# Low parts of 24 of layer 1's projection weights formed during layer 0 and kept in DRAM

## The chip, the cores and the metric

One core of a Trainium2 chip runs the whole kernel. The metric is device time in microseconds (us), less is better. The core has a matrix engine (PE), a vector engine (DVE), a scalar engine (ACT), GpSimd (POOL) and SyncE (SP), which here only issues transfers. Each engine works through its own queue in order, and they wait for one another by semaphores.

## The reference

A two-layer trunk over 256 latent and 256 context tokens of width 1024, in float32. Each layer, cut to what matters here:

```
mod  = silu(c) @ w_ada                  # modulation vectors (scale, shift, gate)
h    = rms_norm(x) * (1 + scale) + shift
p    = h @ w_in                         # q, k, v of three mixers, gates
y_a  = gated_delta_net(p)               # chunked: triangular inverse, then a scan over chunks
y_b  = B * dwconv3(C * h_)              # short gated convolution
y_c  = neighbourhood_attention(p)
x   += gate * ((sum_i sigmoid(g_i) * (y_i @ w_p[i])) @ w_o)      # "merge", then w_o
x   += gate * conv_ffn(rms_norm(x))                              # up projection, conv, down
```

The output is the latent stream after two layers and a last norm.

## The kernel before, in words

**Products in three passes.** Every float32 weight tile is split into a high part (`whi`, rounded to the matrix engine's fp32r type) and a low part (`wlo` = weight minus high part); the activations are split likewise (`hh`, `hl`). A product is three matrix passes: whi·hh, whi·hl, wlo·hh (`mm3`, L175 to L177; the same in `short_conv`, L759). `wsplit` does it for one tile of 128x1024 elements: SP loads it into a buffer `wr` (L135, three buffers), ACT casts it to `whi` (L162), and DVE or POOL subtracts (`wlo`, L165). Every `LOE`-th tile's subtraction goes to POOL: in layer 1's projections every fourth. Layer 0 has three `whi`/`wlo` pairs there and layer 1 four, so the split of a tile starts when PE is done with the tile four (three) before it.

**Stages of a layer.** Projections of the delta net (tiles of `w_in`: k GK 12 to 15, v GV 20 to 23, q GQ 16 to 19), the short convolution's (SCT 24 to 35), the triangular inverse, the scan over chunks, attention, merge, w_o, up projection, down projection. In the profile before, layer 0 has the 24 steps of its merge at 415 to 612 us, `w_o` to 657 us, its up projection to 899 us and its down projection (last tile `pcut`) to 1023 us; layer 1's projections, inverse and scan are at 1026 to 1225 us.

**The inverse.** `X` is formed from the Gram matrices of k (on PE), scaled, transposed into `Bk`; then 30 steps on DVE, each a product into `tm` (L687) and a sum into `Bk` (L688); then a transpose into `Tl` (L689), which the products `py` on PE (L739) read. The compiler weaves other DVE work between these steps: the convolutions of v and q (L350, L351), q's rotation (L522 to L525), the short convolution (`uu`, `cv`), and low parts `wlo`. Meanwhile PE works at the projections of v, q and the short convolution.

**Modulation.** `mod` is not a matrix product after the first part: `ada_all` loads tiles of 512 KB of `w_ada` into two buffers `araw` (L140), one tile ahead, and DVE multiplies and sums each (`aprod`, L241, two per tile). `ada_to` paces these: `ADT` = (0, 32, 16, 32) tiles in layer 0's merge (24 steps, one per block j and branch), up projection (22 steps) and down projection.

**Order.** A scheduler of the program decides the order on each engine from the program's order and the buffers; SP has one queue for nearly all loads. A load whose buffer is not free stands at the queue's head and holds what is behind it.

The step of the merge that paces the work is

```
ps = proj(GT + 3 * j + br, NA_)            # gate, 24 matmuls
w  = wsplit(w_p[l, j, br], 4)              # half a tile
mm3(py[:, OW], w, yhl[br][0], ...)         # pyp, 12 matmuls
ada_to(ADT[0] + (3 * j + bi + 1) * ADT[1] // 24)
```

Of the kernel before, what the change touches and what calls it, by code (L numbers as in the profile page):

```python
# [9 lines left out]
F32 = mybir.dt.float32  # L10
F32R = mybir.dt.float32r
AF = mybir.ActivationFunctionType
ALU = mybir.AluOpType
# [3 lines left out]
P = 128  # L17
# [43 lines left out]
PRE = (12, 13, 14, 15, 20, 21)  # L61

ADT = (0, 32, 16, 32)

CTO, CTD = (2, 0), 1
NC0, NUP, HLE = 4, 2, 0
# [15 lines left out]
def trunk(ctx, tc, xin, cin, cbin, con, par, w_ad0, w_ada, w_in, w_ab, bias, w_p, w_o, w_up, w_dn, out, dbg=None):  # L82
# [62 lines left out]

    cb, wsp = [], []

    def wsplit(src, k, m=128, pool=None, bufs=None, dst=None):
        raw = wraw(src.rearrange("p a b -> p (a b)"), k * m, "wr").rearrange("p (a b) -> p a b", b=m)
        if pool is None:  # L150
            pool, bufs = wsp[0]
        if dst is not None:
            hi, lo = dst
        else:
            hi = pool.tile([P, 8, 128], F32R, tag="whi", bufs=bufs, name="whi")[:, :k, :m]
            lo = pool.tile([P, 8, 128], F32R, tag="wlo", bufs=bufs, name="wlo")[:, :k, :m]
        lo_n[0] += 1
        E_ = G if lo_every[0] and lo_n[0] % lo_every[0] == 0 else V
        na, nb = cuts[0] if k == KD and m == P else (1, 1)
        for i in range(na):  # L160
            c = slice(i * k // na, (i + 1) * k // na)
            A.copy(hi[:, c], raw[:, c])  # L162
        for i in range(nb):
            c = slice(i * k // nb, (i + 1) * k // nb)
            E_.tensor_tensor(lo[:, c], raw[:, c], hi[:, c].bitcast(F32), ALU.subtract)  # L165
        return hi, lo

    def split(hi, lo, src):
        A.copy(hi, src)
        V.tensor_tensor(lo, src, hi.bitcast(F32), ALU.subtract)  # L170
# [84 lines left out]
    def ada_to(n):  # L255

        if not ada_on:
            ada_on.append(1)
            next(ada_gen)
        while ada_at[0] < n:  # L260
            next(ada_gen)
            ada_at[0] += 1
# [105 lines left out]
    for l in range(L):  # L368
# [15 lines left out]

        adf = {}

        def before(q):
            if l == 0:
                if q == 0:
                    adf[0] = ada_first(0, a0p)  # L390
                    next(adf[0])
                next(adf[q])
                if q == 3:
                    nc.sync.dma_start(cb[0], cbin)
                    A.activation(cb[0], cb[0], AF.Silu)
                if q < 3:
                    adf[q + 1] = ada_first(q + 1, a0p)
                    next(adf[q + 1])
            if q == QW[l]:
                raw = wraw(w_ab[l].rearrange("p a b -> p (a b)"), KD * 16, "wr").rearrange("p (a b) -> p a b", b=16)  # L400
                A.copy(wab[:, :, 0:16], raw)
                V.tensor_tensor(wab[:, :, 16:32], raw, wab[:, :, 0:16].bitcast(F32), ALU.subtract)
                for i in range(NT[l]):
                    pre[GK + i] = wsplit(w_in[l, GK + i], KD)
            if q == QX and l == 0:
                for i in range(NT[l], NT[l] + NPX):
                    pre[PRE[i]] = wsplit(w_in[l, PRE[i]], KD, pool=s0p, bufs=NPX)


        first = {}  # L410
# [55 lines left out]
        def proj(ti, n, name="prj", bank=pbank):  # L466
            if ti in first:
                return first.pop(ti)
            w = pre.pop(ti) if ti in pre else wsplit(w_in[l, ti], KD)
            ps = bank(name)  # L470
            mm3(ps[:, : n.stop - n.start], w, hh, hl, KD, n, True, True)
            return ps
# [279 lines left out]

        def short_conv():
            def fproj(ti):
                hi, lo = wsplit(w_in[l, ti], KD)
                ps = pbank("prj")
                for k in range(KD):
                    for i, (a, b) in enumerate(((hi, hh), (hi, hl), (lo, hh))):
                        mm = PE.matmul(ps[:, OW], a[:, k, :], b[:, k, NA_], start=k == 0 and i == 0, stop=k == KD - 1 and i == 2)  # L759
                        if in_scan[0]:  # L760
                            tc.keep_in_program_order(mm)
                        yield ps

            for i in range(4):
                cg = tmp("cg")
                for ps in fproj(SCT + 3 * i):
                    yield
                A.copy(cg[:, OW], ps[:, OW])
                for ps in fproj(SCT + 3 * i + 1):
                    yield  # L770
                uu = tmp("uu")
                V.tensor_tensor(uu[:, OW], ps[:, OW], cg[:, OW], ALU.mult)
                cv = tmp("cv")
                conv3(cv[:, OW].rearrange("p (s t) -> p s t", t=T), uu, lambda tap: pcol(l, "scc", tap * 4 + i), ns)
                for ps in fproj(SCT + 3 * i + 2):
                    yield
                V.tensor_tensor(y_b[:, i], ps[:, OW], cv[:, OW], ALU.mult)
# [199 lines left out]
        with left("at", l) as at:  # L977
            for i in range(4):
# [23 lines left out]
                if i % 2 == 0:  # L1002

                    vh = at.tile([P, 2, KD, P], F32R, tag="vh", bufs=1, name="vh")
                    vl = at.tile([P, 2, KD, P], F32R, tag="vl", bufs=1, name="vl")

                    vst = [wp.tile([P, 2, 4, P], F32R, tag="araw", bufs=2, name="vst") for _ in range(2)]
                    for a in range(2):
                        wsplit(w_in[l, NV + i + a], KD, dst=(vh[:, a], vl[:, a]))
                    for b in range(4):  # L1010
                        ps = pbank("pv")
                        n = slice(b * P, b * P + P)
                        for k in range(KD):
                            PE.matmul(ps[:, : 2 * P], hh[:, k, n], vh[:, :, k, :], start=k == 0, stop=False)
                            PE.matmul(ps[:, : 2 * P], hl[:, k, n], vh[:, :, k, :], start=False, stop=False)
                            PE.matmul(ps[:, : 2 * P], hh[:, k, n], vl[:, :, k, :], start=False, stop=k == KD - 1)
                        pv, vs = ps[:, : 2 * P].rearrange("p (h d) -> p h d", d=64), vst[b // 2][:, b % 2]
                        A.copy(vs[:, :, 0:64], pv)
                        V.tensor_tensor(vs[:, :, 64:P], pv, vs[:, :, 0:64].bitcast(F32), ALU.subtract)
# [57 lines left out]
        for j in range(KD):  # L1077
            acc = tmp("acc")
            for bi, br in enumerate(BRO):
                ps = proj(GT + 3 * j + br, NA_)  # L1080
                gt = tmp("gt", "tg")[:, OW]
                A.activation(gt, ps[:, OW], AF.Sigmoid)
                w = wsplit(w_p[l, j, br], 4)
                if j == 0 and (not last or br == 2 or YSP[br] > 3):
                    ysplit(br)
                py = gbank("pyp")
                mm3(py[:, OW], w, yhl[br][0], yhl[br][1], 4, OW, True, True)
                if bi == 0:
                    V.tensor_tensor(acc[:, OW], py[:, OW], gt, ALU.mult)
                else:  # L1090
                    V.tensor_tensor(gt, py[:, OW], gt, ALU.mult)
                    V.tensor_tensor(acc[:, OW], acc[:, OW], gt, ALU.add)
                if l == 0:
                    ada_to(ADT[0] + (3 * j + bi + 1) * ADT[1] // 24)
            split(mh[:, j], ml[:, j], acc[:, OW])
        RX.close()

# [50 lines left out]
        with right("f", l) as fp:  # L1148
# [22 lines left out]
            for i in range(FT):  # L1171
# [13 lines left out]
                split(fh[:, i], fl[:, i], uv[0])  # L1185
                if not last:
                    ada_to(sum(ADT[:2]) + (i + 1) * ADT[2] // FT)
            cut = 0 if last else CTD
            stat = Stat((fp.tile([P, NW], F32, tag="u", bufs=6, name="sa") if l == 1 else tmp("sa", "tg")), NA_, cut or None)
            norm = None if last else Norm(stat, x, l + 1, "n1g", 1, 0, hh, hl)  # L1190
# [9 lines left out]
            for j in range(KD):  # L1200
                if j == KD - 1 and cut:
                    ada_to(sum(ADT))
                    w = dsplit(j)
                    last_tiles([j], lambda ps, j, n: dmm(ps, j, n, w), 5, norm)
                    break
                ps = pbank("pdn")
                for (k0, kn) in dks:
                    w = wsplit(w_dn[l, j][:, k0 : k0 + kn], kn)
                    mm3(ps[:, OW], w, fh[:, k0 : k0 + kn], fl[:, k0 : k0 + kn], kn, OW, k0 == 0, k0 == 16)
                if not last:  # L1210
                    ada_to(sum(ADT[:3]) + (j + 1) * ADT[3] // KD)
                residual(ps, j, 5, NA_)
                stat.add(x, j)
                if last:
                    A.activation(x[:, j, LAT], x[:, j, LAT], AF.Copy, scale=pcol(0, "fng", j))
# [138 lines left out]
```

## Time and profile before

| | before |
|---|---|
| median of 3 runs | 1673.89 us (1673.30 to 1676.83) |
| profiled execution | 1671.71 us, span 1669.8 us |
| PE busy | 1593.0 us (95%) |
| DVE busy | 1173.2 us (70%) |
| ACT busy | 775.5 us (46%) |
| POOL busy | 232.4 us (14%) |
| mean granted PE clock | 0.977 of full speed |

The span runs from the first to the last instruction of the profiled execution; its time has 1.9 us more around it. The profiled execution lies 2.2 us below the median of the runs.

### The profile page before, as it was taken

What the parts mean: (1) busy time and instruction counts of PE and PEld (TensorE: products, weight loads), DVE (VectorE), ACT (ScalarE), POOL (GpSimd) and SP (SyncE); (2) the same over time, 40 slices, a digit from 0 to 9 for tenths busy, and PEclk for the clock granted to TensorE, in tenths of its full rate; (3) what the DMA queues carried; (4) which work ended last, traced back from release to release, by engine and by line L of the source; (5) the groups of instructions that cost most, each with busy time, mean ns of one, the idle gap of its engine ahead of it and who ended that gap; (6) DMA issues with size and microseconds to landing.
All of it is one profiled execution on the core that took longest, in us unless ns stands there. A gap on an engine that the chain in (4) does not pass through costs nothing.

```text
span 1669.8 us, 26300 instructions
## 1 busy us (share of the span) xinstructions
PE 1593.0 (95%) x10184; PEld 1365.1 (82%) x10184; DVE 1173.2 (70%) x2279; ACT 775.5 (46%) x1361; POOL 232.4 (14%) x181
## 2 busy tenths in 40 slices
PE   5999999999799999999999999979999999999997
PEld 4777788887588888888888888668798899989997
DVE  4697853777777766877778666796767765678753
ACT  3664533566322234544443224653356554466653
POOL 0100311000000000000000001212333033334442
PEclk9999999999899999999999999997999999999999
DMA  9221012312556552444445773122024156546653
GB/s 369 77 76 52 14 51 89 121 36 73 193 173 199 179 177 76 139 130 136 126 130 174 255 227 126 51 89 89 26 87 139 55 169 185 177 153 186 183 174 114
DMA packets 65452, 220.03 MB, mean 132 GB/s; under 512 B 7280, under 2 KB 8688, under 8 KB 65200
## 3 DMA queue, kind: packets, MB, share of 16 engines
q1 hardware_dynamic: 64448, 214.20, 40.2%
q0 software_dynamic: 880, 4.16, 0.8%
q8 instruction: 80, 1.31, 0.3%
q14 instruction: 44, 0.36, 0.1%
HBM read 217.28 MB, written 1.05 MB: 131 GB/s over the span
## 4 chain that ended last, share of the span: by engine, by line
PE 80%; DVE 12%; ACT 4%; issue 2%; DMA 2%; POOL 0%; SPq 0%; DVEq 0%; ACTq 0%; POOLq 0%
PE pup L175 7%; PE pup L176 7%; PE pup L177 7%; PE prj L175 6%; PE prj L176 6%; PE prj L177 6%; PE prj L759 5%; PE pdn L176 3%; PE pdn L177 3%; PE pdn L175 3%; PE pa L787 2%; PE pyp L176 2%; PE pyp L177 2%; PE pyp L175 2%; PE po L787 2%
## 5 line engine op out<-in xcount | busy, mean ns | idle before, releaser
L162 ACT CAST whi<-wr 128x1024 fp32r<-128x1024 f32 (+1 forms) x336 | 313.3, 935 | 505.2 <-PE prj L176 149.0
L165 DVE TENSOR_TENSOR wlo<-wr,whi 128x512 fp32r<-128x512 f32 (+2 forms) x340 | 292.2, 876 | 140.8 <-ACT whi L162 137.7
L175 PE MATMUL prj<-hh,whi 128*128 128x512 f32 (+1 forms) x736 | 261.0, 355 | 8.0 <-DVE v__8934 L351 2.5
L177 PE MATMUL prj<-hh,wlo 128*128 128x512 f32 (+1 forms) x736 | 260.8, 355 | 3.8 <-DVE wlo L165 3.8
L176 PE MATMUL prj<-hl,whi 128*128 128x512 f32 (+1 forms) x736 | 259.9, 353 | 0.0
L175 PE MATMUL pup<-hh,whi 128*128 128x256 f32 (+1 forms) x720 | 239.0, 334 | 1.4 <-ACT hh L340 1.4
L176 PE MATMUL pup<-hl,whi 128*128 128x256 f32 (+1 forms) x720 | 238.8, 333 | 0.0
L177 PE MATMUL pup<-hh,wlo 128*128 128x256 f32 (+1 forms) x720 | 238.7, 333 | 0.0
L165 POOL TENSOR_TENSOR wlo<-wr,whi 128x1024 fp32r<-128x1024 f32 (+2 forms) x80 | 163.7, 2046 | 371.2 <-ACT whi L162 345.9
L175 PEld LDWEIGHTS prj<-hh,whi 128*128 128x128 f32 x736 | 140.3, 191 | 28.1 <-ACT whi L162 3.5
L241 DVE SCALAR_TENSOR_TENSOR aprod<-araw,cb 128x1024 bf16<-128x1024 f32 x128 | 153.4, 1219 | 13.7 <-DMA araw<-w_ada 13.4
L177 PEld LDWEIGHTS prj<-hh,wlo 128*128 128x128 f32 x736 | 140.1, 190 | 23.6 <-DVE wlo L165 4.7
L176 PEld LDWEIGHTS prj<-hl,whi 128*128 128x128 f32 x736 | 140.1, 190 | 19.3 <-issue 3.0
L175 PEld LDWEIGHTS pup<-hh,whi 128*128 128x128 f32 x720 | 136.9, 191 | 14.9 <-ACT hh L340 1.8
L176 PEld LDWEIGHTS pup<-hl,whi 128*128 128x128 f32 x720 | 136.8, 191 | 13.2
L177 PEld LDWEIGHTS pup<-hh,wlo 128*128 128x128 f32 x720 | 136.9, 191 | 13.0
L176 PE MATMUL pdn<-fl,whi 128*128 128x256 f32 (+1 forms) x330 | 109.8, 333 | 0.0
L175 PE MATMUL pdn<-fh,whi 128*128 128x256 f32 (+1 forms) x330 | 109.7, 332 | 0.0
L177 PE MATMUL pdn<-fh,wlo 128*128 128x256 f32 (+1 forms) x330 | 109.7, 332 | 0.0
L497 POOL MEMSET wt<- 128x512 f32 x4 | 2.0, 526 | 697.9 <-PE pcut L176 645.5
L350 DVE SCALAR_TENSOR_TENSOR u<-pup,par,u 128x510 f32<-128x510 f32 (+1 forms) x88 | 53.6, 612 | 47.4 <-ACT u L349 47.4
L759 PE MATMUL prj<-hh,whi 128*128 128x512 f32 (+1 forms) x192 | 69.9, 364 | 0.3 <-DVE q__8924 L351 0.3
(344 smaller groups left out, 3193.3 us busy)
## 6 DMA issues: line engine op xcount, KB each, us to landing
wr<-w_in SPq DMA_DIRECT2D x128, 512.0 KB, 3.8
wr<-w_up SPq DMA_DIRECT2D x88, 512.0 KB, 3.6
araw<-w_ada SPq DMA_DIRECT2D x80, 512.0 KB, 4.0
wr<-w_dn SPq DMA_DIRECT2D x32, 512.0 KB, 4.4
wr<-w_p SPq DMA_DIRECT2D x48, 256.0 KB, 2.7
a<-w_ad SPq DMA_DIRECT2D x16, 512.0 KB, 10.6
wr<-w_o SPq DMA_DIRECT2D x16, 512.0 KB, 3.9
wr<-w_dn SPq DMA_DIRECT2D x16, 384.0 KB, 3.4
```

The source lines that it names most:

```text
L162: A.copy(hi[:, c], raw[:, c])
L165: E_.tensor_tensor(lo[:, c], raw[:, c], hi[:, c].bitcast(F32), ALU.subtract)
L175: PE.matmul(ps, hi[:, i, :], xh[:, i, n], start=first and i == 0, stop=False)
L176: PE.matmul(ps, hi[:, i, :], xl[:, i, n], start=False, stop=False)
L177: mm = PE.matmul(ps, lo[:, i, :], xh[:, i, n], start=False, stop=last and i == k - 1)
L241: V.scalar_tensor_tensor(prod, nxt, 1.0, cb[0][:, i], ALU.mult, ALU.mult, accum_out=macc[:, i, b : b + 1])
L350: V.scalar_tensor_tensor(dst[:, :, 1:T], pv[:, :, 0 : T - 1], wc(0), dst[:, :, 1:T], ALU.mult, ALU.add)
L497: G.memset(t, 0.0)
L759: mm = PE.matmul(ps[:, OW], a[:, k, :], b[:, k, NA_], start=k == 0 and i == 0, stop=k == KD - 1 and i == 2)
L787: i_ = PE.matmul(*a, **k)
```

## The change

For 24 tiles of layer 1's `w_in` (list `LOD`) the low part is formed in layer 0. A generator `lo_all` takes a tile at a time: SP loads it into an `araw` buffer, ACT casts each half into a buffer `lh`, DVE subtracts each half in place, and POOL's queue stores the 512 KB into a DRAM tile `lod`. `LDT` = (0, 10, 14, 0) paces it: 10 tiles over the merge's 24 steps and 14 over the up projection's 22, each call just behind `ada_to`. In layer 1 these tiles go through `win`: SP loads the tile as before, ACT casts it to `whi`, and SP loads `wlo` from `lod`; there is no subtraction. They no longer advance the counter that sends every fourth subtraction to POOL.

```
+LOD = (12, 13, 14, 15, 20, 21, 22, 23, 16, 17, 18, 19) + tuple(range(24, 36))
+LDT = (0, 10, 14, 0)
...
+    def lo_all():
+
+        for ti in LOD:
+            yield
+            raw = araw(w_in[L - 1, ti].rearrange("p a b -> p (a b)"))
+            for i in range(2):
+                c = slice(512 * i, 512 * i + 512)
+                t = tmp("lh").bitcast(F32R)
+                A.copy(t, raw[:, c])
+                V.tensor_tensor(raw[:, c].bitcast(F32R), raw[:, c], t.bitcast(F32), ALU.subtract)
+            lod[ti] = tc.dram_tile([P, KD * P], F32, name=f"lod{ti}")
+            G.dma_start(lod[ti], raw)
+        yield
...
-    def wsplit(src, k, m=128, pool=None, bufs=None, dst=None):
+    def wsplit(src, k, m=128, pool=None, bufs=None, dst=None, lod_=None):
...
+        if lod_ is not None:
+            A.copy(hi, raw)
+            nc.sync.dma_start(lo.bitcast(F32), lod_.rearrange("p (a b) -> p a b", b=m))
+            return hi, lo
         lo_n[0] += 1
         E_ = G if lo_every[0] and lo_n[0] % lo_every[0] == 0 else V
...
+        def win(ti, **a):
+            return wsplit(w_in[l, ti], KD, lod_=lod.get(ti) if last else None, **a)
...
-            w = pre.pop(ti) if ti in pre else wsplit(w_in[l, ti], KD)
+            w = pre.pop(ti) if ti in pre else win(ti)
...
                     ada_to(ADT[0] + (3 * j + bi + 1) * ADT[1] // 24)
+                    lo_to(LDT[0] + (3 * j + bi + 1) * LDT[1] // 24)
...
                     ada_to(sum(ADT[:2]) + (i + 1) * ADT[2] // FT)
+                    lo_to(sum(LDT[:2]) + (i + 1) * LDT[2] // FT)
```

Three places in the engines' orders follow; the changed program's line numbers are about 30 higher (L138 is L135 before, L143 is L140, L195 is L165, L720 is L687, L721 is L688, L722 is L689).

SP's queue in layer 0's merge, before: loads of half tiles `w_p` and tiles `w_in` for the merge, and of `w_ada`.

```order
L140 DMA araw<-w_ada 128x1024 x2
L135 DMA wr<-w_p 128x512
L135 DMA wr<-w_in 128x1024
L140 DMA araw<-w_ada 128x1024 x2
L135 DMA wr<-w_p 128x512
L135 DMA wr<-w_in 128x1024
L135 DMA wr<-w_p 128x512
L135 DMA wr<-w_in 128x1024
```

The same place of the change.

```order
L143 DMA araw<-w_ada 128x1024 x2
L138 DMA wr<-w_p 128x512
L143 DMA araw<-w_in 128x1024
L138 DMA wr<-w_in 128x1024
L138 DMA wr<-w_p 128x512
L143 DMA araw<-w_ada 128x1024 x2
L138 DMA wr<-w_in 128x1024
L143 DMA araw<-w_ada 128x1024
```

The load `araw<-w_in` of a tile to be stored stands in the queue among the merge's own loads; the next loads of `w_ada` take the buffers in turn, and one of them waits for the store from that tile's buffer.

DVE in layer 1, at the end of the 30 steps of the inverse, before.

```order
L687 TENSOR_TENSOR tm<-Bk 128x210
L772 TENSOR_TENSOR uu<-prj,cg 128x256
L688 TENSOR_TENSOR Bk<-Bk,tm 128x10x21
L165 TENSOR_TENSOR wlo<-wr,whi 128x1024
L687 TENSOR_TENSOR tm<-Bk 128x198
L350 SCALAR_TENSOR_TENSOR cv<-uu,par_74,cv 128x255
L688 TENSOR_TENSOR Bk<-Bk,tm 128x9x22
L351 SCALAR_TENSOR_TENSOR cv<-uu,par_74,cv 128x255
L687 TENSOR_TENSOR tm<-Bk 128x184
L165 TENSOR_TENSOR wlo<-wr,whi 128x1024
L688 TENSOR_TENSOR Bk<-Bk,tm 128x8x23
```

The end of the same steps in the change, up to the transpose into `Tl`.

```order
L666 TENSOR_TENSOR attn<-gram,E 128x256
L721 TENSOR_TENSOR Bk<-Bk,tm 128x2x29
L666 TENSOR_TENSOR attn<-gram,E 128x256
L720 TENSOR_TENSOR tm<-Bk 128x30
L666 TENSOR_TENSOR attn<-gram,E 128x256
L721 TENSOR_TENSOR Bk<-Bk,tm 128x30
L805 TENSOR_TENSOR uu<-prj,cg 128x256
L722 STREAM_TRANSPOSE Tl<-Bk 128x32x32
```

All eight subtractions `wlo` between the 30 steps are gone; the Gram products' scaling (`attn`) and the second `uu`, which waits for a matmul of tile 28, have come to stand ahead of the transpose, where before `uu` stood behind it.

POOL in layer 1 from the projections to the scan, before.

```order
L165 TENSOR_TENSOR wlo<-wr,whi 128x1024
L640 TENSOR_TENSOR gm<-cst,cols 128x512 x2
L165 TENSOR_TENSOR wlo<-wr,whi 128x1024
L640 TENSOR_TENSOR gm<-cst,cols 128x512 x2
L663 TENSOR_TENSOR X<-X,cols 128x512 x2
L683 MEMSET Bk 128x32
L165 TENSOR_TENSOR wlo<-wr,whi 128x1024 x5
L849 TENSOR_TENSOR S<-S,cols 128x2x128 x12
L165 TENSOR_TENSOR wlo<-wr,whi 128x1024
```

The same stretch of the change.

```order
L673 TENSOR_TENSOR gm<-cst,cols 128x512 x4
L696 TENSOR_TENSOR X<-X,cols 128x512 x2
L716 MEMSET Bk 128x32
L882 TENSOR_TENSOR S<-S,cols 128x2x128 x24
L946 TENSOR_TENSOR oacc<-oacc,ot 128x256 x4
```

Eight subtractions of POOL are gone; what is left is its share of the delta net.

## Rows read from the trace of the kernel before

**Rows 1.** The page: busy engines, and the chain of waits.

```profile
PE 1593.0 (95%) x10184; PEld 1365.1 (82%) x10184; DVE 1173.2 (70%) x2279; ACT 775.5 (46%) x1361; POOL 232.4 (14%) x181
...
PE 80%; DVE 12%; ACT 4%; issue 2%; DMA 2%; POOL 0%; SPq 0%; DVEq 0%; ACTq 0%; POOLq 0%
```

**Rows 2.** Busy time by stretch: us, PE, PEld, DVE, ACT, POOL, clock, DMA.

```profile
1050.00:1100.00 50.00, 44.71 (x259) 31.75 (x258) 37.93 (x84) 26.92 (x38) 8.57 (x8) 1.00 0.18 57
1100.00:1150.00 50.00, 36.93 (x323) 32.08 (x323) 46.66 (x96) 25.21 (x40) 11.41 (x4) 0.86 0.32 103
1150.00:1225.00 75.00, 72.78 (x661) 59.30 (x659) 45.24 (x118) 25.95 (x64) 20.86 (x28) 0.86 0.09 29
```

**Rows 3.** DVE's groups, 1088 to 1146 us: count, busy, mean ns, idle before.

```profile
L687 DVE TENSOR_TENSOR tm<-Bk 128x30 f32<-128x30 f32 (+14 forms) x30 | 15.7, 524 | 0.4
...
L165 DVE TENSOR_TENSOR wlo<-wr,whi 128x1024 fp32r<-128x1024 f32 x8 | 9.7, 1217 | 0.0
L522 DVE TENSOR_TENSOR r<-q__8924,cst 64x512 f32<-64x512 f32 x2 | 3.5, 1746 | 0.1
```

**Rows 4.** DVE's groups in layer 0's inverse, 95 to 148 us.

```profile
L687 DVE TENSOR_TENSOR tm<-Bk 128x30 f32<-128x30 f32 (+14 forms) x30 | 9.9, 328 | 0.6
```

**Rows 5.** POOL's timeline in the inverse: start, duration.

```profile
1139.31 2.52 POOL L165 TENSOR_TENSOR wlo<-wr,whi 128x1024 fp32r<-128x1024 f32 x1 [4.96 <-ACT whi L162]
```

**Rows 6.** DVE's timeline from 1139 us: start, duration.

```profile
1139.58 2.35 DVE L687 TENSOR_TENSOR tm<-Bk 128x84 f32<-128x84 f32 x1
```

**Rows 7.** PE's timeline where `py` begins.

```profile
1145.26 2.50 PE L739 MATMUL py<-Tl,X 32*32 32x32 f32 x64 [3.57 <-DVE Tl L689]
```

**Rows 8.** Busy time by stretch: layer 1 from the inverse to `py`.

```profile
1083.00:1145.26 62.26, 46.70 (x326) 40.07 (x324) 58.40 (x117) 32.51 (x50) 11.57 (x5) 0.92 0.32 102
```

**Rows 9.** Busy time by stretch: `py` and `pz` in layer 0, then layer 1.

```profile
147.50:163.50 16.00, 16.00 (x277) 13.64 (x277) 10.79 (x24) 6.38 (x10) 0.00 (x0) 0.79 0.11 35
...
1145.20:1164.00 18.80, 18.74 (x285) 18.13 (x286) 8.85 (x22) 6.16 (x10) 0.76 (x1) 0.55 0.10 31
```

**Rows 10.** Busy time by stretch: layer 0's merge with `w_o`, then its up projection.

```profile
440.00:657.00 217.00, 217.00 (x998) 181.00 (x997) 153.87 (x274) 65.29 (x91) 0.00 (x0) 0.99 0.53 171
657.00:897.00 240.00, 239.40 (x1106) 200.02 (x1106) 185.81 (x306) 107.72 (x146) 0.00 (x0) 1.00 0.41 128
```

**Rows 11.** SP's waits in layer 0's merge: us in total, times, longest.

```profile
SPq L140 <- DVE aprod L241: 94.3, 32, 6.4
```

**Rows 12.** DVE's groups in layer 0's merge, 420 to 660 us.

```profile
L241 DVE SCALAR_TENSOR_TENSOR aprod<-araw,cb 128x1024 bf16<-128x1024 f32 x64 | 75.8, 1219 | 0.3 <-DMA araw<-w_ada 0.3
L165 DVE TENSOR_TENSOR wlo<-wr,whi 128x512 fp32r<-128x512 f32 x84 | 54.4, 687 | 21.4 <-ACT whi L162 21.2
```

**Rows 13.** ACT's groups in the same stretch.

```profile
L162 ACT CAST whi<-wr 128x512 fp32r<-128x512 f32 x21 | 13.1, 622 | 87.1 <-PE prj L176 81.5 <-DVE aprod L241 4.4 <-PE pyp L176 1.2
```

**Rows 14.** Transfers: KB each, median us from issue to landing.

```profile
wr<-w_in SPq DMA_DIRECT2D x128, 512.0 KB, 3.8
...
araw<-w_ada SPq DMA_DIRECT2D x80, 512.0 KB, 4.0
...
wr<-w_p SPq DMA_DIRECT2D x48, 256.0 KB, 2.7
...
yout<-x SPq DMA_DIRECT2D x4, 256.0 KB, 2.9
```

**Rows 15.** POOL's issues of transfers `bt`: ns, least, median, most.

```profile
L984 POOL DMA_DIRECT2D bt<-bias x8: 536/553/582, 291.7 to 1315.5; - x8
```

**Rows 16.** The page: GB/s in 40 slices of the span.

```profile
GB/s 369 77 76 52 14 51 89 121 36 73 193 173 199 179 177 76 139 130 136 126 130 174 255 227 126 51 89 89 26 87 139 55 169 185 177 153 186 183 174 114
```

**Rows 17.** PE's timeline at the start of layer 1.

```profile
1027.12 0.38 PE L429 MATMUL prj<-hh,wlo 128*128 128x256 f32 x1 [0.76 <-DVE wlo L165]
...
1028.64 0.28 PE L429 MATMUL prj<-hh,whi 128*128 128x256 f32 x1
1028.76 0.28 PE L429 MATMUL prj<-hl,whi 128*128 128x256 f32 x1
```

More of the change, by code (lines that the diff above doesn't have):

```diff
@@ L146, in trunk, with lo_to @@
     cb, wsp = [], []
-    def wsplit(src, k, m=128, pool=None, bufs=None, dst=None):
+    lod = {}
+    def lo_all():
[10 more added lines that the diff above has]
+        yield
+    lo_gen, lo_at = lo_all(), [-1]
+    def lo_to(n):
+        while lo_at[0] < n:
+            next(lo_gen)
+            lo_at[0] += 1
+    def wsplit(src, k, m=128, pool=None, bufs=None, dst=None, lod_=None):
         raw = wraw(src.rearrange("p a b -> p (a b)"), k * m, "wr").rearrange("p (a b) -> p a b", b=m)
@@ L403, in before @@
                 for i in range(NT[l]):
-                    pre[GK + i] = wsplit(w_in[l, GK + i], KD)
+                    pre[GK + i] = win(GK + i)
             if q == QX and l == 0:
                 for i in range(NT[l], NT[l] + NPX):
-                    pre[PRE[i]] = wsplit(w_in[l, PRE[i]], KD, pool=s0p, bufs=NPX)
+                    pre[PRE[i]] = win(PRE[i], pool=s0p, bufs=NPX)
         first = {}
@@ L754, in fproj @@
             def fproj(ti):
-                hi, lo = wsplit(w_in[l, ti], KD)
+                hi, lo = win(ti)
                 ps = pbank("prj")
@@ L1008, in trunk @@
                     for a in range(2):
-                        wsplit(w_in[l, NV + i + a], KD, dst=(vh[:, a], vl[:, a]))
+                        win(NV + i + a, dst=(vh[:, a], vl[:, a]))
                     for b in range(4):
@@ L1202, in trunk @@
                     ada_to(sum(ADT))
+                    lo_to(sum(LDT))
                     w = dsplit(j)
@@ L1211, in trunk @@
                     ada_to(sum(ADT[:3]) + (j + 1) * ADT[3] // KD)
+                    lo_to(sum(LDT[:3]) + (j + 1) * LDT[3] // KD)
                 residual(ps, j, 5, NA_)
```

## The prediction

> **What bounds the kernel now.** I read the page first. PE is busy 95% of the span, and the chain of waits goes through PE for 80% and through DVE for 12% [rows 1]: where PE is full, no other engine's work costs anything, and what can be won lies in the stretches where PE waits. The change touches two kinds of stretch, so I read the busy time of both.
>
> In layer 0's merge with w_o, PE is busy 217.00 of 217 us, and in the up projection 239.40 of 240; DVE has 153.87 us (71%) and 185.81 us (77%) there, and POOL nothing [rows 10]. Here the change adds work, all of it under a full PE. In layer 1, from 1050 to 1225 us, PE is short of full by 5.3, 13.1 and 2.2 us, 20.6 us in all; DVE is the busiest just where PE is emptiest (46.66 of 50 us, PE 36.93) and the granted clock falls to 0.86 [rows 2]. That is the inverse: `py` begins at 1145.26 us, after PE has waited 3.57 us for the transpose into `Tl` [rows 7]. Over the whole stretch from 1083 us to there PE is busy 46.70 of 62.26 us and DVE 58.40 [rows 8]. So DVE's chain to `Tl` ends last, and every us that leaves it moves `py`.
>
> **Layer 1: what leaves the chain.** In the inverse DVE runs eight `wlo` subtractions, 9.7 us, with no idle time ahead of them [rows 3]. They go. POOL runs four more in the same stretch, the last of 2.52 us [rows 5], and these hold DVE up: the product at 1139.58 us, which POOL's last one overlaps from 1139.31 us, takes 2.35 us [rows 6]. What this comes to is read from two groups: the 30 products into `tm` take 15.7 us in layer 1 [rows 3] and the same 30 shapes 9.9 us in layer 0 [rows 4], 5.8 us more; the two `L522` take 3.5 us [rows 3], where a subtraction of the same 512 elements takes 0.69 [rows 12], 2.1 us more. In all 9.7 + 5.8 + 2.1 = 17.6 us, a little less where the instructions overlapped at their ends: 17.
>
> Then PE is next. Its 46.70 us of work stay, so `py` can't come more than 62.26 - 46.70 = 15.6 us earlier at the clock granted now (0.92 [rows 8]); at full clock the same work takes 46.70 x 0.92 = 43 us, and the bound is 19. DVE with 58.40 - 17 = 41 us and about 3 us of waits stands at 44. The two are level; I take **16 us**, bounds 8 (if the loads or PE come late, below) and 19. Before the inverse (the k tiles, the decay columns, `X`) I count nothing: four subtractions less on DVE and two less on POOL, against a last k tile that comes later behind POOL's `gm`; bounds -2 and +3.
>
> After `py`, layer 1 takes 18.80 us for `py` and `pz` at a mean clock of 0.55 and layer 0 16.00 us for them at 0.79 [rows 9]. PE was idle 13.1 us in the 50 us before [rows 2]; if it is nearly full there, the clock should fall less. The difference is 2.8 us; I take **2.5**, bounds 0 and 2.8 + 2.2 (PE's idle time in the scan [rows 2], where two subtractions of DVE and two of POOL go too).
>
> **Layer 1: what comes in.** Each of the 24 low parts is now a load of 512 KB by SP, 3.8 us after its issue as for `w_in` [rows 14]. It waits for the same buffer as the subtraction did, and both the cast and the load can run ahead by four tiles. At the start of the layer PE now waits 0.76 us for a subtraction [rows 17]; a load of 3.8 us in its place, whose buffer comes free while `pcut` still runs, lands at about that time: zero, bounds -1 and +1.5.
>
> **Layer 0: what it costs.** Per tile ACT has two casts of 0.62 us [rows 13], DVE two subtractions of 0.69 us [rows 12]: 48 of each, 30 us on ACT and 33 us on DVE. In the merge 10 tiles take 14 us of DVE, in the up projection 14 take 19 us; idle there are 29% of the merge's 197 us, 57 us, and 23% of 240 us, 54 us [rows 10]. The cover is PE's full queue. It breaks only if DVE falls so far behind that a `wlo` of the merge itself comes late: the whole lead is a step of 197 / 24 = 8.2 us, less the cast (1.2 us as two halves) and three half subtractions (2.1 us), 5 us.
>
> What could make DVE late is the buffer, not the arithmetic. A `w_ada` tile holds an `araw` buffer for its load, 4.0 us [rows 14], and two products of 1.22 us [rows 12]: 6.4 us. A stored tile holds it for the load, some 2.5 us of casts and subtractions, and the store. No store of 512 KB is in the trace. The nearest rows are `yout`, 256 KB to DRAM in 2.9 us, and `w_p`, 256 KB from DRAM in 2.7 us, so writing costs 0.2 us more than reading, and 512 KB read take 3.8 to 4.0 us [rows 14]: I take 4.1, and 0.6 for POOL's issue [rows 15], bounds 2.9 and 8 (twice a load). In all 11 us. 32 + 10 tiles in the merge then use 32 x 6.4 + 10 x 11 = 315 of the two buffers' 394 us, 80% where it was 52%; in the up projection 16 x 6.4 + 14 x 11 = 256 of 480 us, 53%. So the up projection is free, and in the merge a tile will at times be waited for: DVE for the tile's own load (up to 4.0 us, since the load can start only when the products just ahead are done), then for the `w_ada` tile behind the store. Today DVE loses 0.3 us in all to these loads [rows 12], while SP stands 94.3 us at the head of its queue for `aprod` [rows 11]; behind it there are the merge's own `wr` loads. At 2 us a tile the wait is 20 us, with the 14 us of work 34 of the 57 idle, so most is absorbed; where two such steps follow one another some reaches PE. I take **3 us**, bounds 0 and 10.
>
> The Trainium skill speaks against this part: DMA: Bandwidth & Descriptors, section Anatomy of one DMA, says that a transfer counts as done only when the target memory confirms the last byte, and that this can take surprisingly long when the target is HBM. The trace agrees only in direction, 0.2 us between the two rows of 256 KB. That section's fit (2.0 us and bytes over 436 GB/s) would give an estimate of 3.2 us for such a store in place of 4.1, and the sum would stay.
>
> **Sum.** 16 + 2.5 - 3 = 15.5 us off the profiled execution's 1671.7: 1656.2. That execution lay 2.2 us below the median of the runs, so the median comes to **1658 us**.
>
> **The rivals.**
> - *The loads become the bound in layer 1.* A tile of the short convolution is 24 matmuls, started every 0.12 us [rows 17]: 2.9 us, in which it needs 1 MB now: 364 GB/s, where the best slice of the trace shows 369 and the next best 255 [rows 16]. At 255 a tile takes 4.1 us, 1.2 us late each; of some ten tiles in a row the four buffers hide the first ones, so up to 8 us are lost and the chain gains 8. With 3 us of cost and no clock regained: 5 us, 1669. For it: these bytes are new in a stretch that moved 103 GB/s [rows 2]; against it: SP may run four tiles ahead, and the inverse's start has slack.
> - *POOL's stores are issued late.* DVE and POOL hold each other up (above). If each store's issue stands behind the DVE instruction then running, up to 1.22 us [rows 12], the ten of the merge cost 12 us where they are on the path, instead of 3: 18.5 - 12 = 6.5, 1667. Against it: POOL's eight issues so far took 536 to 582 ns, none of them longer [rows 15], so its chance is small. The Trainium skill, SBUF — State Buffer, section SBUF: two separate sides, describes such a trap, with a copy on DVE that locks GpSimd out while it would write a transfer's descriptors; no run so far shows a store from POOL under DVE's work.
> - *Slower: the merge starves.* The place is SP's queue in the merge: the load of a `w_ada` tile waits there for the store out of its buffer, and `wr` loads of the merge stand behind it. If DVE's lag per stored tile is not caught up in the steps between (2.4 steps with some 2.4 us idle each, 5.8 us, against a load of 4.0, 1.4 of work and the next tile's load, 4.0 again: 9.4), PE loses 3.6 us per tile, 36 us in the merge, and the time is 1674 - 18.5 + 36 = 1691. It decides from 1.85 us per tile on. For it: 80% use of the buffers and a queue in order. Against it: 5 us of lead, and a store that is issued at once.
> - *No change.* PE's own waits for k's norms and the Gram products end later by as much as the inverse gets shorter, or the stages meet a lower clock: 1674.
>
> **How the numbers follow.** The forecast's own case, 1652 to 1664, has 0.60; the loads as the bound 0.15; late stores 0.08; the starved merge 0.11; no change 0.06. From 1649 (all upper bounds of layer 1, 19 + 5, and no cost) to 1669 the range holds the first three, 0.83. A measurement here tells 0.2%, 3.3 us, from no change: faster 0.82, same 0.07, slower 0.11.
>
> **What the profile after would show.** If the steps are right: no `wlo` on POOL before the scan and none on DVE in the inverse; the 30 products into `tm` back at about 10 us; `py` some 16 us after the place that a shift of the earlier stages gives it, at a PE that is nearly full before; in the merge DVE at some 78% with waits for `araw` of 10 to 25 us, and PE short of full by at most a few us. The sum is wrong if PE's idle time in the merge exceeds 10 us, if matmuls of layer 1 wait for loads of `lod`, or if `py` still waits for DVE as long as before.

## The result, and the profile after

| | before | the change |
|---|---|---|
| median | 1673.6 us (4 runs) | 1649.08 us (4 runs, 1644.47 to 1652.23) |
| ratio | | 0.9845, 95% interval 0.9826 to 0.9864 |
| profiled execution, span | 1671.71 us, 1669.8 us | 1652.23 us, 1650.5 us |

The change takes 24.5 us off the median, where 15.5 were forecast; 1649.08 us stands at the lower end of the range, and the ratio puts the gain at 22.8 to 29.1 us. The way it went was forecast, its size was not: the gain is more than half as large again, and by the medians larger than the 24 us to which the prediction's upper bounds for layer 1 add up with no cost at all.

The page of the change begins with the busy times; [rows 1] is its counterpart. PE and DVE do nearly the same as before in a span that is 19 us shorter.

```profile
PE 1588.7 (96%) x10184; PEld 1362.4 (83%) x10184; DVE 1167.6 (71%) x2311; ACT 799.6 (48%) x1409; POOL 224.6 (14%) x197
```

**Where the time went.** The profiled execution of the change was the slowest of its four, so I compare stages, not spans. The markers are matmuls that both programs have: the end of `pcut` (the last of layer 0), the beginning of `py` and the end of `pz` (just behind the inverse), and the last `pv` (in layer 1's attention). From `pcut` to the last `pv` PE has 2004 matmul records in either trace. This is the busy time of that stretch, before and then the change (columns as in [rows 2]: length; PE, PEld, DVE, ACT, POOL busy; clock; DMA share; GB/s):

```profile
1023.40:1308.70 285.30, 262.15 (x2004) 221.32 (x2003) 208.79 (x467) 146.48 (x286) 68.56 (x61) 0.94 0.25 81
```

```profile
1027.70:1290.80 263.10, 256.24 (x2004) 218.00 (x2003) 175.29 (x451) 146.19 (x286) 47.99 (x53) 0.97 0.40 134
```

The stretch is 22.2 us shorter, in two parts. PE's idle time falls from 285.30 - 262.15 = 23.2 us to 263.10 - 256.24 = 6.9 us: 16.3 us. And the same 2004 matmuls keep PE busy for 256.24 in place of 262.15 us, 5.9 us less, with a mean granted clock of 0.97 in place of 0.94 (1 is 2.4 GHz, 0.5 is 1.2 GHz). These lengths repeat in the profiles of the experiments below: e1, whose layer 1 is that of before, has 285.6 us in the stretch, 262.5 of them busy; e2, e7 and e8, whose layer 1 does the change's work, have 263.0, 261.9 and 258.6 us, busy 256.5, 255.3 and 251.9. Behind the last `pv` the change's profile is 1.4 us shorter, ahead of `pcut`'s end 4.3 us longer (1027.7 against 1023.4 us); the first experiment shows that this last is no cost of the change.

Parted at the beginning of `py`, the same gain is 16.6 us ahead of it and 163.4 - 157.8 = 5.6 us behind it. Ahead of it PE's idle time falls from 19.3 to 4.8 us, although it does 15 more matmuls there (before, then the change):

```profile
1023.40:1145.26 121.86, 102.56 (x681) 82.54 (x680) 100.87 (x210) 67.53 (x101) 24.33 (x17) 0.96 0.27 87
1027.70:1133.00 105.30, 100.49 (x696) 82.59 (x695) 74.89 (x197) 67.28 (x102) 8.66 (x11) 1.00 0.58 204
```

**The inverse.** DVE's groups in the inverse of the change, answering to [rows 3]:

```profile
L720 DVE TENSOR_TENSOR tm<-Bk 128x30 f32<-128x30 f32 (+14 forms) x30 | 9.8, 328 | 0.5
...
L555 DVE TENSOR_TENSOR r<-q__9166,cst 64x512 f32<-64x512 f32 x2 | 1.4, 686 | 0.1
```

The 30 products take 9.8 us (15.7 before), the first operations of q's rotation 1.4 (3.5), and there is no `wlo`. `py` begins 105.3 us behind `pcut`'s end, where it was 121.9: 16.6 us earlier. PE still waits there for `Tl`, for 0.85 us where [rows 7] has 3.57:

```profile
1133.00 1.17 PE L772 MATMUL py<-Tl,X 32*32 32x32 f32 x35 [0.85 <-DVE Tl L722]
```

But the wait for `Tl` was not PE's longest ahead of `py`. That was for the squares of q (`pss` on PE reads what ACT's `sqk` forms from q, once DVE has rotated it): 8.9 us in two waits before, the longest 7.7, and 1.5 in the change. The rotation is woven into the same chain on DVE and was held up with it: its first operation took 2.80 us beside POOL's subtraction from 1113.32 us, the same operation for the other half of q 0.69.

```profile
PE pss L535 <- ACT sqk L534: 8.9, 2, 7.7
```

```profile
PE pss L568 <- ACT sqk L567: 1.5, 1, 1.5
```

**The clock.** Two stretches of before and of the change show where the 5.9 us come from. Before, PE was busy only 4.32 of the 10 us from 1120 us (the wait of 7.7 us), and the granted clock there was 0.64; it was 0.77 in 15 us of the scan, about a wait of 1.4 us for DVE.

```profile
1120.00:1130.00 10.00, 4.32 (x12) 1.73 (x12) 9.88 (x22) 1.84 (x5) 0.00 (x0) 0.64 0.18 58
1185.00:1200.00 15.00, 13.56 (x94) 10.87 (x90) 11.23 (x27) 4.57 (x11) 6.54 (x8) 0.77 0.11 36
```

In the change PE is busy 8.54 of the 10 us from 1120 us and 14.86 of the 15 in the scan, and the clock is 1.00 in both:

```profile
1120.00:1130.00 10.00, 8.54 (x82) 6.43 (x81) 7.83 (x30) 5.10 (x11) 0.00 (x0) 1.00 0.84 309
1185.00:1200.00 15.00, 14.86 (x132) 11.47 (x132) 11.10 (x32) 8.00 (x21) 4.20 (x8) 1.00 0.01 2
```

In all, the clock was 0.50 in three stretches of before (1122.7 to 1133.0, 1146.6 to 1163.7 and 1191.0 to 1197.8 us), with PE busy for 31 us of them; of the change only one is left (1134.5 to 1151.6 us), 17 us. It is the one about `py` and `pz`, which run at 0.55 as before. So the prediction had looked for the higher clock in the wrong place:

```profile
1133.00:1147.40 14.40, 14.40 (x264) 13.82 (x265) 6.85 (x19) 5.08 (x8) 0.00 (x0) 0.55 0.30 106
```

**Layer 0.** In the merge with w_o, and then in the up projection, the change shows this (the counterpart of [rows 10]); PE is short of full by 0.6 us in each, the first a wait for a low part of the merge's result that [rows 10] doesn't have:

```profile
443.00:660.00 217.00, 216.39 (x996) 180.18 (x996) 166.11 (x293) 76.41 (x111) 5.33 (x10) 1.00 0.65 219
660.00:900.00 240.00, 239.40 (x1101) 200.38 (x1101) 197.94 (x329) 118.14 (x169) 6.38 (x12) 0.99 0.55 179
```

DVE is at 77% and 82% of the stretch, up from 71% and 77%. What it waits for is in its groups from 420 to 660 us (as [rows 12]): 6.8 us for `araw` loads, 9.6 us for the casts `lh`, while its idle time for other casts fell from 21.2 to 11.0 us. The waits took the place of others.

```profile
L271 DVE SCALAR_TENSOR_TENSOR aprod<-araw,cb 128x1024 bf16<-128x1024 f32 x64 | 76.2, 1219 | 6.8 <-DMA araw<-w_ada 6.8
L195 DVE TENSOR_TENSOR wlo<-wr,whi 128x512 fp32r<-128x512 f32 x83 | 53.8, 685 | 11.1 <-ACT whi L192 11.0
L162 DVE TENSOR_TENSOR araw<-araw,lh 128x512 fp32r<-128x512 f32 x20 | 12.9, 688 | 9.6 <-ACT lh L161 9.6
```

SP's queue in the same window stands 16.0 us for stores, nine times, and for `aprod` 102.2 us, where [rows 11] has 94.3:

```profile
SPq L143 <- DVE aprod L271: 102.2, 32, 6.7
SPq L143 <- DMA lod<-araw: 16.0, 9, 5.7
```

The store itself, 512 KB, lands 3.2 us after its issue, and POOL's issue takes 0.53 us each time (the first row is from the list of transfers, as [rows 14]; the second gives the operations on `lod`, least, median and most in ns, as [rows 15]):

```profile
lod<-araw POOLq DMA_DIRECT2D x24, 512.0 KB, 3.2
```

```profile
L164 POOL DMA_DIRECT2D lod<-araw x24: 531/531/542, 446.7 to 914.5; - x24
```

### The profile page after: what moved, and what is told of

The parts are those of the page before. It is cut to its first block, busy times and chain, and to the rows that moved or that the text cites. A ratio compares the mean times of both kernels' runs of the same rounds, so it can differ in the third digit from the quotient of the medians.

```text
span 1650.5 us, 26543 instructions
## 1 busy us (share of the span) xinstructions
PE 1588.7 (96%) x10184; PEld 1362.4 (83%) x10184; DVE 1167.6 (71%) x2311; ACT 799.6 (48%) x1409; POOL 224.6 (14%) x197
## 5 line engine op out<-in xcount | busy, mean ns | idle before, releaser
L192 ACT CAST whi<-wr 128x1024 fp32r<-128x1024 f32 (+2 forms) x312 | 288.2, 927 | 432.6 <-PE prj L206 99.7
L195 DVE TENSOR_TENSOR wlo<-wr,whi 128x512 fp32r<-128x512 f32 (+2 forms) x324 | 273.0, 859 | 124.2 <-ACT whi L192 118.8
L195 POOL TENSOR_TENSOR wlo<-wr,whi 128x1024 fp32r<-128x1024 f32 (+2 forms) x72 | 142.7, 1983 | 300.4 <-ACT whi L192 289.6
L205 PEld LDWEIGHTS prj<-hh,whi 128*128 128x128 f32 x736 | 139.7, 190 | 25.7 <-ACT whi L192 2.8
L164 POOL DMA_DIRECT2D lod<-araw x24 | 12.8, 532 | 520.8 <-DVE araw L162 520.8
```

Source lines behind the costliest of these rows:

```text
L164: G.dma_start(lod[ti], raw)
L205: PE.matmul(ps, hi[:, i, :], xh[:, i, n], start=first and i == 0, stop=False)
```

## The experiments

All runs in one table; each ratio is to runs of the kernel before on the same chip, with its 95% interval.

| run | median us | ratio |
|---|---|---|
| the change | 1649.08 | 0.9845 (0.9826 to 0.9864) |
| e1_cost_only | 1674.90 | 0.9994 (0.9983 to 1.0006) |
| e2_gain_only | 1652.44 | 0.9844 (0.9822 to 0.9867) |
| e3_late_pool | 1653.17 | 0.9865 (0.9848 to 0.9881) |
| e4_late_dve | 1651.34 | 0.9856 (0.9837 to 0.9874) |
| e5_before_late_dve | 1674.78 | 1.0000 (0.9986 to 1.0014) |
| e6_before_no_pool | 1662.49 | 0.9932 (0.9917 to 0.9947) |
| e7_merge_all | 1703.83 | 1.0172 (1.0151 to 1.0192) |
| e8_store_sp | 1651.46 | 0.9862 (0.9841 to 0.9883) |
| e9_pool8 | 1659.31 | 0.9912 (0.9895 to 0.9929) |
| e10_dve16 | 1658.96 | 0.9909 (0.9892 to 0.9926) |
| e11_lo_dve_l1 | 1649.65 | 0.9838 (0.9817 to 0.9859) |
| e12_lo_dve | 1649.97 | 0.9847 (0.9823 to 0.9870) |

**Cost alone, gain alone.** The first leaves layer 1 as it was; the second forms one tile and reads it 24 times.

```
-            return wsplit(w_in[l, ti], KD, lod_=lod.get(ti) if last else None, **a)
+            return wsplit(w_in[l, ti], KD, **a)                       # e1
...
-        for ti in LOD:
+        for ti in LOD[:1]:                                            # e2
-LDT = (0, 10, 14, 0)
+LDT = (0, 1, 0, 0)
+            return wsplit(w_in[l, ti], KD, lod_=lod[LOD[0]] if last and ti in LOD else None, **a)
```

Expected of e1:

> The 24 low parts are formed and stored in layer 0 as in the change, but layer 1 does its own split as before and never reads them. If the layer 0 part costs about what the trace of the change shows (1 us between the first pyp and the end of pcut, beside a difference that was there before the merge), the time is that of before, 0 to +2 us. The prediction's 3 us would give +3. If the merge loses what the starved-merge rival says, +10 us and more, and the change's gain in layer 1 would then be that much larger than its trace shows.

Expected of e2:

> Only one low part is formed and stored in layer 0, and layer 1 loads that one 24 times in place of the 24, so the output is not the reference's and the layer 0 work of 23 tiles is left out. If layer 0's work is free, the time is that of the change, 23 to 25 us under before. If it costs 3 us as predicted, 3 us less than the change; if the cost is hidden elsewhere and large, more.

The work in layer 0 costs nothing that can be measured: -1.0 us, with an interval of -2.8 to +1.0. Its profile has the merge, w_o and the up projection (from the first `pyp` to the first `pwo`, `pup` and `pdn`) at 195.5, 46.7 and 243.4 us, the change's at 195.3, 46.6 and 243.4; before's are 196.5, 45.7 and 242.0. The 2 us more in the last two can't be told from what executions differ by: e11 and e12 below, with the same work, have 46.0 and 46.7, and 242.0 both. e2, without that work, has the change's own ratio. In e1 `pcut` ends at 1029.5 us and in e5 and e6, whose layer 0 is that of before, at 1027.7 and 1028.9: the 1023.4 us of before's profile were a quick execution of layer 0, by some 4 us. The gain lies in layer 1, all of it.

**The last four tiles.** At first I took the shorter scan (pz to the last `po` 65.3 us before, 59.6 in the change) for the work of POOL's subtraction there, which coincides with the wait of 1.4 us and the dip of the clock. e3 and e4 leave tiles 32 to 35 out of the list; e5 is the kernel before with two subtractions given to DVE. `on` is the engine of a tile's subtraction (G is POOL, V is DVE).

```
+LOD = (12, 13, 14, 15, 20, 21, 22, 23, 16, 17, 18, 19) + tuple(range(24, 32))
+LDT = (0, 10, 10, 0)
+            on = (V, G, V, G)[ti - 32] if last and 32 <= ti < 36 else None    # e3
+            on = (V, V, V, V)[ti - 32] if last and 32 <= ti < 36 else None    # e4
...
+            return wsplit(w_in[l, ti], KD, on=V if last and ti in (33, 35) else None, **a)   # e5, nothing stored
```

Expected of e3:

> The change without tiles 32 to 35, whose subtractions run in the scan: 32 and 34 on DVE, 33 and 35 on POOL, as before. Theory A (POOL's subtraction in the scan holds up DVE's wt, PE runs dry, and the clock falls): 3 to 5 us slower than the change, with a stretched wt and a clock under 1 in the scan. Theory B (the scan is shorter only because PE comes to it fuller and with fewer projections left): 0 to 1 us slower.

Expected of e4:

> As the run before, but the four subtractions of tiles 32 to 35 all on DVE. Theory A: most of it comes back, 0 to 1.5 us slower than the change, no stretched wt. Theory B: the same as the run before. If any subtraction in the scan costs its own time on the path, 3 to 5 us slower here too.

Expected of e5:

> The kernel before, with the subtractions of tiles 33 and 35 (POOL's two in layer 1's scan) on DVE. Theory A (POOL's subtraction in the scan holds up DVE's wt, PE waits 1.4 us, the clock falls): no wait of pa for rr, the scan's clock up from 0.92 to about 0.96, the scan 3 to 4 us shorter, ratio about 0.998. Theory B (the scan is shorter in the change because it has some 15 projection matmuls less and comes after a fuller PE): within 1 us of before.

Theory A, that POOL's subtraction in the scan makes DVE late and PE run dry, falls as the reason of the gain. In e5 the wait of `pa` is gone and the scan's clock is 0.97, as theory A asked, but the time is that of before; the low clock came earlier (0.50 in `py` and `pz`), and the whole stretch from `pcut` to `pv` has its length again, 285.1 us:

```profile
1027.70:1312.80 285.10, 265.04 (x2004) 222.41 (x2003) 208.66 (x468) 145.95 (x286) 63.25 (x59) 0.93 0.26 81
```

e3 and e4 lose 3.3 and 1.8 us against the change by their ratios, not clear of its interval, and 0.6 and 1.6 us in that stretch (263.7 and 264.7 us). So the subtractions inside the scan are worth little, though e3's 3.3 us don't exclude theory A's 3 by themselves. What the scan gained is then mostly what PE brought to it: 15 fewer matmuls left to do (462 in place of 477), and a clock without the dip (0.92 to 0.96 in the scan).

**POOL's part and DVE's part.** e6 is the kernel before with all 24 subtractions on DVE. e9 stores only the 8 tiles that POOL had (every fourth up to tile 27, from there every second), DVE keeping its 16; e10 stores those 16, POOL keeping its 8.

```
+            return wsplit(w_in[l, ti], KD, on=V if last and ti in LOD else None, **a)   # e6, nothing stored
...
+LOD = (15, 23, 19, 27, 29, 31, 33, 35)                                                  # e9, the rest on=V
+LDT = (0, 4, 4, 0)
...
+LOD = (12, 13, 14, 20, 21, 22, 16, 17, 18, 24, 25, 26, 28, 30, 32, 34)                  # e10, the rest on=G
+LDT = (0, 8, 8, 0)
```

Expected of e6:

> The kernel before, with all 24 subtractions of these tiles on DVE, none on POOL. If what POOL holds up in the inverse is 5.8 + 2.1 us as read from the groups, the 30 products into tm are back at 9.9 us and the rotation's L522 at 1.4, against four more subtractions of 1.22 us: py 3 us earlier; with theory A for the scan 6 us in all, ratio 0.996 to 0.998. If the stretched instructions are no cost of POOL's, py is 5 us later and the ratio 1.002 or more.

Expected of e9:

> Only the 8 tiles whose subtraction POOL had (15, 19, 23, 27, 29, 31, 33, 35) come from DRAM; the other 16 are subtracted by DVE as before. If POOL's subtractions cost the 7.9 us that the prediction read from stretched instructions, and the clock little: 8 to 11 us under before, ratio 0.993 to 0.995. If they cost what the run with all 24 on DVE suggests (11 us gained there with eight subtractions more on DVE): 15 to 21 us under before, ratio 0.988 to 0.991.

Expected of e10:

> The other half: the 16 tiles that DVE subtracted come from DRAM, POOL keeps its 8. By the prediction's terms DVE loses 9.7 us in the inverse: 10 to 12 us under before, ratio 0.993 to 0.994. If POOL's subtractions are the larger part, 4 to 9 us under before, ratio 0.995 to 0.998; the gains of this run and the one before then need not add up to the change's 25 us, since either leaves PE less idle time.

e6 gains 11.4 us although DVE has eight subtractions more; I had expected 3 to 6. Its 26 products seen in the window of the inverse take 340 ns each, and nothing is stretched:

```profile
L720 DVE TENSOR_TENSOR tm<-Bk 128x130 f32<-128x130 f32 (+14 forms) x26 | 8.8, 340 | 0.2
```

The stretch of the two halves, e9 and then e10:

```profile
1025.20:1298.00 272.80, 258.58 (x2004) 218.40 (x2003) 195.42 (x466) 145.57 (x284) 47.63 (x53) 0.96 0.31 100
```

```profile
1026.20:1297.20 271.00, 258.27 (x2004) 218.89 (x2003) 188.11 (x450) 145.22 (x284) 67.21 (x61) 0.96 0.35 115
```

Each half alone gains some 15 us of the change's 24.5 (14.7 and 15.2 by the ratios, 12.5 and 14.3 in the stretch). e9 is just under the 15 to 21 us expected; e10's 10 to 12 was too low. `py` begins 112.2 and 112.8 us behind `pcut`'s end, 9.7 and 9.1 us earlier than before; the rest of the gain lies behind it. The two do not add up: PE's idle time of 23.2 us falls to 14.2 and 12.7 by either and to 6.9 by both, since there is less and less of it to take, and each half also brings back a part of the clock (PE busy 3.6 and 3.9 us less). The longest wait, that for the squares of q, is 5.6 us in either half and 1.5 only where both are gone. e6 shows besides that `py` is no full measure: there it begins 121.4 us behind `pcut`'s end, 0.4 us earlier than before, but PE has done 747 matmuls by then in place of 681, and the gain shows up behind the scan, where that work is missing.

**The merge's limit, and the store's queue.**

```
-LDT = (0, 10, 14, 0)
+LDT = (0, 24, 0, 0)                                                  # e7
...
-            G.dma_start(lod[ti], raw)
+            nc.sync.dma_start(lod[ti], raw)                          # e8
```

Expected of e7:

> The change with all 24 tiles formed in the merge, none in the up projection. Each stored tile holds its buffer for 4.0 (load) + 2.5 + 3.2 us (store as now measured), 9.7 us: 32 x 6.4 + 24 x 9.7 = 438 us of the two buffers' 394, over the full use. If the buffers decide, as the starved-merge rival says, the merge gets at least 22 us longer, 10 to 25 us slower than the change. If DVE's arithmetic decides (24 x 1.4 = 34 of 57 us idle), the time is that of the change.

Expected of e8:

> The change with the stores on SP's queue instead of POOL's. The store then stands at SP's head until DVE has subtracted, with the merge's and the up projection's own loads behind it. If that lead matters, 2 to 10 us slower than the change; if the loads have enough lead, the same. If POOL's issue were late under DVE's work, faster.

e7 is the starved merge, made on purpose: the merge takes 220 us in place of 196 and w_o 71.6 in place of 46.6, 50 us more, and the kernel ends 55 us behind the change. DVE waits for casts of stored tiles 36.2 us and for `w_ada` loads 25.7 us from 415 to 680 us. The casts are late because their tile is: ACT waits 93.9 us for the loads into `araw`. PE waits for the products that come late behind them:

```profile
ACT lh L161 <- DMA araw<-w_in: 93.9, 20, 12.0
DVE araw L162 <- ACT lh L161: 36.2, 18, 4.7
DVE aprod L271 <- DMA araw<-w_ada: 25.7, 10, 4.1
```

```profile
PE pyp L205 <- DVE acc L1122: 21.0, 3, 8.8
PE pwo L205 <- ACT gt L1115: 13.9, 1, 13.9
```

The use of the two buffers, worked out with the store as measured, is 32 x 6.4 + 10 x 9.7 = 302 of 394 us (77%) in the change, at no cost, and 111% in e7, at 50 us. That it was the excess of 44 us over two buffers, 22 us, is not borne out: the loss is more than twice that. I read it so that DVE, held up in its own order, is late for everything behind; no run separates that.

e8 is 2.8 us behind the change by its ratio, and their intervals overlap: SP's queue can carry the stores too, and there is no gain in it, so POOL's issues held nothing up that can be measured.

**Other subtractions on POOL.** e11 and e12 ask whether POOL holds DVE up elsewhere.

```
-LOE = ((0, 0, 3, 0), (4, 2, 3, 2))
+LOE = ((0, 0, 3, 0), (4, 0, 0, 0))                                   # e11
+LOE = ((0, 0, 0, 0), (4, 0, 3, 2))                                   # e12
```

Expected of e11:

> The change, with the rest of layer 1's subtractions that POOL has (attention, merge, the later products) on DVE. If POOL's subtractions hold DVE up there too where PE waits, 1 to 4 us faster than the change. If PE is full there (it is, but for some 3 us in 210), the same, or slower where DVE is now late.

Expected of e12:

> The change, with layer 0's subtractions that POOL has (in attention) on DVE. The same question in layer 0: the same time within 2 us if PE is full there, 1 to 4 us faster if POOL's subtractions hold up what PE waits for.

Both have the change's time within the intervals (1.2 us faster and 0.3 slower by the ratios), so what DVE and POOL do to each other there costs nothing that can be measured. No version was found that is clearly better than the change.

## Why the prediction was right in its way and too small

The steps that failed are two terms of the sum: the 2.5 us after `py`, which measured 5.6 and lie above their own upper bound of 5.0, and the 3 us for the merge, which measured nothing.

- *DVE's chain to `Tl` sets `py`, and PE is next:* right in that what left DVE moved `py`, 16.6 us for the 16 taken. It was not the transpose alone that PE stood for: its longest wait there was for the squares of q, 7.7 us, which the prediction does not name. It hung on the same DVE instructions and fell with them. PE's idle time in the whole stretch fell by 16.3 us.
- *17.6 us leave the chain, 9.7 of DVE's own and 7.9 of what POOL holds up:* the rows were read rightly (9.8 us and 1.4 us after), and at `py` the two prices nearly hold: DVE's sixteen alone move it 9.1 us (e10), POOL's eight alone 9.7 (e9). But they price only what lies ahead of `py`. In all, POOL's eight alone are worth 15 us (e9), and 11 even when DVE does them (e6); DVE's sixteen alone 15 us (e10). Why POOL's eight are worth that much more than 7.9 us is settled only in part: there is the clock, there is the wait for q, and PE got 66 more matmuls done before `py` in e6, whose order on PE the scheduler changed; how much is that order I didn't separate.
- *2.5 us after `py`:* the first term that was mis-sized: it measured 5.6. The term took its size from a higher clock in `py` and `pz`, and that did not come: they were granted 0.55 again and took 14.6 us where they had taken 14.8 (the 18.8 us of [rows 9] reach 4 us past the last `pz`). Instead the dip of the clock in the scan went, PE's idle time behind `py` fell from 3.9 to 2.1 us, and 15 matmuls had been done ahead of it. Over the whole stretch the higher clock shows as the same matmuls in 5.9 us less of busy time, a part of it ahead of `py`, where PE no longer runs dry.
- *3 us for the merge:* the second term that was mis-sized; it is zero (e1: -2.8 to +1.0 us). DVE did wait for `araw`, 16 us in the merge and w_o against the 20 worked out, but PE's lead took all of it. The store took 3.2 us and not 4.1; the Trainium skill's fit in DMA: Bandwidth & Descriptors, section Anatomy of one DMA, which gave the estimate of 3.2, was nearer than the value that I took from the rows, and its long delay for a target in HBM did not show: the load of the same tile took 3.6 us.
- The sum by the measured terms is 16.6 + 5.6 - 0 = 22.2 us in the stretch, a little under the 22.8 to 29.1 of the ratio. These are single executions: runs of one kernel differ by some 8 us, and part of that is the clock. In e8's profile `py` and `pz` were granted 0.90 and took 10.2 us, in the change's 0.55 and 14.6, so the clock's part of the gain is no fixed number.
- *The rivals:* the loads were no bound. From 1120 to 1130 us they moved 309 GB/s, and no matmul waited for one. POOL's stores were issued on time, 531 to 542 ns under a DVE that is busy 77% and more. The starved merge was a real mechanism with the wrong threshold for 10 tiles; with 24 it came.

## What to carry to other kernels

A subtraction on a second engine is not priced by that engine's idle time: POOL was idle three quarters of the stretch, and its eight subtractions cost as much as DVE's sixteen, and the instructions on DVE that they had stretched were short again without them. A chain is set by all that waits for it: read every wait of the engine that it feeds, not the last one alone (7.7 us for the squares of q against 3.57 for `Tl`). Where PE runs dry between full stretches, look at the slower clock about the gap as well as at the idle time (here 5.9 us to 16.3). Work that is moved under a full engine can be free up to a limit that buffers set before arithmetic does: two buffers at 77% cost nothing here, at 111% 50 us, although DVE's added work (34 us) would have fitted into its idle time (57 us).

## What the runs showed of the hardware

- DVE stands for whole instructions of POOL: a product on DVE that takes 0.25 us in the change took 2.35 us beside a POOL subtraction of 2.52 us and ended 0.1 us behind it [rows 5, 6]. The Trainium skill, SBUF — State Buffer, section SBUF: two separate sides, says that DVE and GpSimd lock a pair of ports for the length of an instruction, also where the DVE operation has two inputs in SBUF and GpSimd's one reads SBUF; the trace agrees, and with POOL's subtractions gone the 30 products are back at 328 ns from 524. The stores' issues on POOL were not touched by DVE's work (531 to 542 ns).
- The granted clock is not fixed by the program: with the same work in layer 1, `py` and `pz` had 0.55 in the change's profile and 0.90 in e8's. And a dip can go without gain: in e5 that of the scan went (0.92 to 0.97), while `py` and `pz` had 0.50 in place of 0.55.
